# Two of the next four experts' activations placed between the value blocks of a dense expert stage

## The chip, the cores and the metric

The kernel runs on one core of one Trainium2 chip. The metric is device time in microseconds (us) of one execution. Before the change the median of three runs is 3982.32 us (3981.56 to 3986.05).

## The reference

One inference layer over nine blocks of 128 tokens (eight of a prompt, one of eight sampled sequences of 16 tokens): a mixer and then PEER, an expert layer of 16384 single-neuron experts. Only PEER's second half is touched by the change. For each token, 8 heads choose 16 experts each by product keys, and

```
u_sel = expert_u[e_idx]
act = gelu(einsum('thkd,td->thk', u_sel, xt))
out = einsum('thk,thkd->td', g * act, expert_v[e_idx])
```

with g the softmax of the 16 chosen scores. The mixer's recurrent half has a causal convolution and a scan, whose states of the sampled sequences come in as inputs (st_conv, st_lru) and go out updated (conv_s, lru_s).

## The kernel before, in words

The nine blocks are computed in three groups (mixer, scores, choice of experts), up to about 2010 us. Then PEER is done in two ways at once. Four blocks are *gathered*: for each of 128 choices, GpSimd issues an indirect transfer of one row of expert_u or expert_v per token (line 910), and VectorE reduces it (lines 937, 958). Five blocks are *dense*: all 16384 experts are computed for their 640 tokens, with a table G of weights that is zero where an expert was not chosen. The 16384 experts are 128 rows of 128; in the code, and in what follows, such a row of 128 is "an expert e" of the dense stage, and four of them (ECH) are a chunk c; there are 32 chunks.

The dense stage (function dense) has two pieces per chunk.

- u_phase(e, gt) is one activation. It loads expert_u's weights into raw, splits them into a high and a low half (hi on ScalarE, lo on VectorE: fp32 products are made of three matmuls), makes 2 x 24 matmuls into two PSUM tiles pp, applies gelu into wf (ScalarE, line 1043), multiplies by the weights in gt (VectorE, line 1045), and splits the result into wh (ScalarE) and wl (VectorE). wf has one buffer, wh and wl have five each (ECH + 1), gt has one buffer: the gt of a chunk can be loaded only when the fourth activation of the chunk before has been multiplied.
- v_phase(c, ws, vs) is the value product of a chunk, for the five token blocks in the order 2, 0, 3, 1, 4: 24 matmuls each (four experts, three products, two halves of 512 columns). Blocks 0 and 1 keep their sums in PSUM over the whole stage. Blocks 2, 3 and 4 share the one PSUM tile that is left, and after each of them VectorE adds the tile to acc (line 1077), which frees it. load_v(e) loads and splits an expert's values into vh and vl (four buffers each), which are free again when the last block of a chunk has read them.

Before the change the program's order per chunk is: activations 2 to 4 of the chunk, each followed by load_v; load_g of the next chunk; the first activation of the next chunk; v_phase; load_v for that first one.

The program's order is not the order on the engines. The Tile framework plans it beforehand (line 1280): on each engine, what comes first in the program has priority, and where that is not ready by the planner's reckoning, later work is put in. On the chip each engine then goes strictly by this plan. The gathers come last in the program, so their vector operations stand where VectorE had a gap in the plan.

The two lines that decide the order between the chunks' pieces:

```
nxt = [u_phase((c + 1) * ECH, gt)]
v_phase(c, ws, vs, nf)
```

Of the kernel before, what the change touches and what calls it, by code (L numbers as in the profile page):

```python
# [10 lines left out]
F32 = mybir.dt.float32  # L11
# [47 lines left out]
ECH = 4  # L59
AT_ONCE = (0, 5)  # L60
LAG = 3
FLOW = ((0,) * 5, (0.2, 0.26, 0.26, 0.26, 0.26), (0.13, 0.26, 0.3, 0.26, 0.26))


# [5 lines left out]
def kernel(ctx, tc, a):  # L70
    nc = tc.nc
    V, S, P, T = nc.vector, nc.scalar, nc.gpsimd, nc.tensor

    const = ctx.enter_context(tc.tile_pool(name="const", bufs=1))
# [27 lines left out]
    h_last = const.tile([128, 8], F32, name="h_last")  # L102
    V.memset(xr_last, 0.0)
    V.memset(h_last, 0.0)
    st_conv = const.tile([128, 8, 8, 3], F32, name="st_conv")
    nc.scalar.dma_start(st_conv, a["st_conv"])
    st_lru = const.tile([128, 8, 8], F32, name="st_lru")
    nc.scalar.dma_start(st_lru, a["st_lru"])
    conv_s = const.tile([128, 8, 8, 3], F32, name="conv_s")
    rms = const.tile([128, NB], F32, name="rms")  # L110
    lru_s = const.tile([128, 8, 8], F32, name="lru_s")

    xt_d = {b: dr_p.tile([128, D], F32, name=f"xt_d{b}") for b in range(NB)}
    s_d = [dr_p.tile([8, 128, len(g), 2, 128], F32, name=f"s_d{n}") for n, g in enumerate(GROUPS)]
# [133 lines left out]
    def mixer(mp, gi, t0, xn):  # L248
# [5 lines left out]
        samp = SB in blocks  # L254
# [6 lines left out]
        left = [sum(p * w for p, w in zip(parts, PACE[gi]))]  # L261
# [4 lines left out]
        def pair(name):  # L266
            return mp["big"].tile([128, 2, KT, Tn], F32, name=name, tag="big")
# [21 lines left out]


        ol = pair("ol")

        def lru_in(c):
            ps = pj(("w_in", CX + c), xn)
# [56 lines left out]
        def lru_scan(c, gb, xc, tr, h, av):  # L351
            V.scalar_tensor_tensor(xc, xc, 0.5, tr, op0=ALU.mult, op1=ALU.mult)
            V.tensor_tensor_scan(h[:, 0:Tp], av[:, 0:Tp], xc[:, 0:Tp], h_last[:, c:c + 1],
                                 op0=ALU.mult, op1=ALU.add)
            V.tensor_copy(h_last[:, c:c + 1], h[:, Tp - 1:Tp])
            if samp:
                bs = xc[:, Tp:Tn].rearrange("p (s t) -> p s t", s=8)[:, :, 0:1]
                as_ = av[:, Tp:Tn].rearrange("p (s t) -> p s t", s=8)[:, :, 0:1]
                ah = sm_p.tile([128, 8, 1], F32, name="ah")
                V.tensor_tensor(ah, as_, st_lru[:, c].unsqueeze(2), op=ALU.mult)  # L360
                V.tensor_tensor(bs, bs, ah, op=ALU.add)
                V.memset(as_, 0.0)
                V.tensor_tensor_scan(h[:, Tp:Tn], av[:, Tp:Tn], xc[:, Tp:Tn], 0.0,
                                     op0=ALU.mult, op1=ALU.add)
                V.tensor_copy(lru_s[:, c].unsqueeze(2),
                              h[:, Tp:Tn].rearrange("p (s t) -> p s t", s=8)[:, :, 15:16])
            V.scalar_tensor_tensor(h, h, 0.5, gb, op0=ALU.mult, op1=ALU.mult)
            split(ol[:, 0, c, :], ol[:, 1, c, :], h)

        ahead = deque([lru_in(0), lru_in(1)])  # L370
        for c in range(0, KT, 2):
            sts = []
            for e in range(2):
                if c + e + 2 < KT:
                    ahead.append(lru_in(c + e + 2))
                gb = lru_gelu(c + e)
                sts.append((gb, *lru_gates(c + e, *ahead.popleft())))
            for st in sts:
                S.activation(st[2], st[2], ACTF.Sqrt)
            for e in range(2):  # L380
                lru_scan(c + e, *sts[e])

        stage[0] = phase[1] = 1

# [633 lines left out]
    def dense(dp):  # L1018
        nd = len(DENSE)
        Td = nd * 128  # L1020
        xt2 = dp["x"].tile([128, 2, KT, Td], F32, name="xd")
        accs = [None, None]
        for i, b in enumerate(DENSE):
            x = (w_p.tile([128, D], F32, name="xt", tag="raw", bufs=RAW_BUFS) if i < RAW_BUFS else
                 w_p.tile([128, D], F32, name="xt", tag="lo"))
            nc.sync.dma_start(x, xt_d[b])
            transpose_in(x, xt2, i * 128, dp["ps"])

        ps_p = dp["pp"]
        ps_s = dp["ps"]  # L1030

        def u_phase(e, gt):
            tick(2)
            hi, lo = load_split(a["peer_ut"][e], raw=u0 if e == 0 else None)
            wh = dp["w"].tile([128, Td], F32, name="wh")
            wl = dp["w"].tile([128, Td], F32, name="wl")
            w = dp["w"].tile([128, Td], F32, name="wf", bufs=1)
            for m in range(0, Td, Td // 2):
                c1 = slice(m, m + Td // 2)
                ps = ps_p.tile([128, Td // 2], F32, name="pp", tag="pp")  # L1040
                for k in range(KT):
                    mm3(ps, (hi[:, k, :], lo[:, k, :]), (xt2[:, 0, k, c1], xt2[:, 1, k, c1]), k == 0, k == KT - 1)
                S.activation(w[:, c1], ps, ACTF.Gelu_apprx_tanh)  # L1043
            w3 = w.rearrange("p (c t) -> p c t", t=32)
            V.tensor_tensor(w3, w3, gt[:, :, e % ECH, :], op=ALU.mult)  # L1045
            split(wh, wl, w)
            return wh, wl

        def load_v(e):
            vh = dp["v"].tile([128, D], F32, name="vh")  # L1050
            vl = dp["v"].tile([128, D], F32, name="vl")
            return load_split(a["peer_v"][e], vh, vl, (128, D))

        def load_g(c):
            gt = dp["g"].tile([128, NCH, ECH, 32], F32, name="gt")
            nc.sync.dma_start(gt, G_d[:, :, c * ECH:(c + 1) * ECH, :].rearrange("n p i t -> p n i t"))
            return gt

        kept = [ps_s.tile([128, 2, 512], F32, name="S", tag="S") for _ in range(2)]

        def v_phase(c, ws, vs, nf=None):
            for i in (2, 0, 3, 1, 4):
                held = i < len(kept)
                po = kept[i] if held else ps_s.tile([128, 2, 512], F32, name="S", tag="S")
                c1 = slice(i * 128, i * 128 + 128)
                for n, ((wh, wl), (vh, vl)) in enumerate(zip(ws, vs)):
                    for q, (l, r) in enumerate(((wh, vh), (wh, vl), (wl, vh))):
                        for m in range(2):
                            T.matmul(po[:, m, :], r32(l[:, c1]), r32(r[:, m * 512:m * 512 + 512]),  # L1069
                                     start=(n == 0 and q == 0 and (c == 0 or not held)),  # L1070
                                     stop=(n == ECH - 1 and q == 2 and (c == nch - 1 or not held)))
                if held and c == nch - 1:
                    acc = w_p.tile([128, D], F32, name="acc", tag="lo")
                    nc.sync.dma_start(acc, x2_d[DENSE[i]])
                    accs[i] = acc
                if not held or c == nch - 1:
                    V.tensor_tensor(accs[i], accs[i], po.rearrange("p m c -> p (m c)"), op=ALU.add)  # L1077
                if c == nch - 1:
                    finish(DENSE[i], accs[i], w_p.tile([128, D], F32, name="yo", tag="hi"), nf)

        nch = 128 // ECH
        gt = load_g(0)
        ws, vs = [u_phase(0, gt)], [load_v(0)]
        for i in range(2, nd):
            acc = dp["x"].tile([128, D], F32, name=f"acc{i}")
            nc.sync.dma_start(acc, x2_d[DENSE[i]])
            accs.append(acc)
        for c in range(nch):
            for e in range(c * ECH + 1, (c + 1) * ECH):
                ws.append(u_phase(e, gt))  # L1090
                vs.append(load_v(e))
            nxt = []
            if c + 1 < nch:
                gt = load_g(c + 1)
                nxt = [u_phase((c + 1) * ECH, gt)]
            nf = None
            if not nxt:
                nf = w_p.tile([128, D], F32, name="nf", tag="raw", bufs=RAW_BUFS)
                nc.sync.dma_start(nf, a["norm_final"].to_broadcast([128, D]))
            v_phase(c, ws, vs, nf)  # L1100
            ws = nxt
            vs = [load_v((c + 1) * ECH)] if nxt else []

    mp = {nm: es_m.enter_context(tc.tile_pool(name=nm, bufs=bufs, reuse_waits="tile"))
          for nm, bufs in (("big", 2), ("s", S_BUFS), ("kv", 2), ("b", 2), ("c", 4))}
# [67 lines left out]
    es_m.close()  # L1173
    with ExitStack() as es:
        dp = {nm: es.enter_context(tc.tile_pool(name=f"d{nm}", bufs=bufs, reuse_waits="tile"))
              for nm, bufs in (("x", 1), ("w", ECH + 1), ("v", ECH), ("g", 1))}
        for nm, bufs in (("pp", 2), ("ps", 3)):
            dp[nm] = es.enter_context(tc.tile_pool(name=f"d{nm}", bufs=bufs, space=bass.MemoryType.PSUM))
        phase[0] = 3
        dense(dp)  # L1180
# [2 lines left out]
            pass  # L1183
    nc.sync.dma_start(a["conv_p"], xr_last)
    nc.sync.dma_start(a["lru_p"], h_last)
    nc.sync.dma_start(a["conv_s"], conv_s)
    nc.sync.dma_start(a["lru_s"], lru_s)


def layout(inp):  # L1190
# [109 lines left out]
```

## Time and profile before

| | before |
|---|---|
| median of three runs | 3982.32 us |
| profiled execution | 3979.21 us, span 3977.3 us |
| TensorE (PE) busy | 3647.0 us, 92% |
| VectorE (DVE) busy | 3042.7 us, 77% |
| ScalarE (ACT) busy | 1618.2 us, 41% |
| GpSimd (POOL) busy | 1405.4 us, 35% |
| moved by DMA | 1208.05 MB, mean 304 GB/s |

Times in a profile are microseconds from the first instruction. L1077 is line 1077 of the kernel. A matmul's busy time overlaps the next one's, so rates of TensorE are read from starts. "idle before <- X" names what ended the idle time: the work or transfer X that the engine waited for. PEclk is the mean clock granted to TensorE as a share of full speed.

### The profile page before, as it was taken

How to read it: one execution, taken by the hardware profiler on the slowest of the kernel's cores; microseconds unless marked ns; L12 is line 12 of the kernel's file. 1: busy time of each engine (PE TensorE's matmuls, PEld its weight loads, DVE VectorE, ACT ScalarE, POOL GpSimd, SP SyncE). 2: the span in 40 equal slices, each digit the busy share in tenths (PEclk: the TensorE clock that was granted, in tenths of full speed). 3: DMA queues.
4: the chain of work that ended last, by engine and by line, in shares of the span. 5: the costliest groups of instructions: out<-in, count | busy, mean ns of one | idle time of the engine just before them, and what ended most of it. 6: DMA issues, size and time to landing. Idle time of an engine off the chain costs nothing. (4 is left out here: it accounts for less than half of the span.)

```text
span 3977.3 us, 59539 instructions
## 1 busy us (share of the span) xinstructions
PE 3647.0 (92%) x21775; PEld 3264.7 (82%) x21775; DVE 3042.7 (77%) x6332; ACT 1618.2 (41%) x2699; POOL 1405.4 (35%) x1094
## 2 busy tenths in 40 slices
PE   8998899898998999888888889999999899999998
PEld 7877799876887987778888778888888888888887
DVE  8433357868675879987778888888877887877887
ACT  7554346556644845665532122222222222222222
POOL 0000000122221023222106555655664655655653
PEclk9999999999998999999999999999999999999999
DMA  7778887888899898879968888989888889888986
GB/s 260 253 243 317 296 283 271 327 308 269 316 385 331 294 346 292 292 281 360 379 203 308 306 287 296 320 314 343 311 305 293 322 313 332 311 304 305 331 311 233
DMA packets 470358, 1208.05 MB, mean 304 GB/s; under 512 B 41008, under 2 KB 199088, under 8 KB 467504
## 3 DMA queue, kind: packets, MB, share of 16 engines
q1 hardware_dynamic: 292496, 638.23, 45.2%
q0 software_dynamic: 147456, 536.94, 37.8%
q10 hardware_dynamic: 30112, 29.09, 2.1%
q8 instruction: 170, 2.79, 0.3%
q14 instruction: 124, 1.02, 0.1%
HBM read 1066.15 MB, written 137.94 MB: 303 GB/s over the span
## 5 line engine op out<-in xcount | busy, mean ns | idle before, releaser
L910 POOL DMA_INDIRECT row<-peer_u,ei x512 | 698.0, 1363 | 1260.5 <-DVE row L937 631.3
L910 POOL DMA_INDIRECT row<-peer_v,ei x512 | 683.3, 1334 | 828.7 <-DVE x L958 525.4
L958 DVE SCALAR_TENSOR_TENSOR x<-row,q,x 128x1024 f32<-128x1024 f32 x512 | 655.3, 1280 | 27.2 <-DMA row<-peer_v,ei 20.8
L175 PE MATMUL pp<-xd,hi 128*128 128x320 f32 x2048 | 639.8, 312 | 31.9 <-ACT wf L1043 26.9
L937 DVE SCALAR_TENSOR_TENSOR row<-row,xt 128x1024 f32<-128x1024 f32 x512 | 613.6, 1217 | 66.1 <-DMA row<-peer_u,ei 64.4
L176 PE MATMUL pp<-xd,hi 128*128 128x320 f32 x2048 | 637.5, 311 | 0.3 <-DVE xd L142 0.3
L177 PE MATMUL pp<-xd,lo 128*128 128x320 f32 x2048 | 636.8, 311 | 0.0
L175 PE MATMUL pp<-xn,hi 128*128 128x384 f32 x1344 | 477.4, 356 | 19.1 <-ACT st L1011 7.8
L1069 PE MATMUL S<-vh,wh 128*128 128x512 f32 x1280 | 410.0, 402 | 62.2 <-DVE acc L1077 54.0
L177 PE MATMUL pp<-xn,lo 128*128 128x384 f32 x1344 | 459.4, 343 | 2.1 <-DMA lo<-lo_w_in 2.1
L176 PE MATMUL pp<-xn,hi 128*128 128x384 f32 x1344 | 460.6, 343 | 0.1
L1069 PE MATMUL S<-vh,wl 128*128 128x512 f32 x1280 | 401.1, 402 | 27.6 <-DVE wl L142 27.6
L175 PEld LDWEIGHTS pp<-xd,hi 128*128 128x128 f32 x2048 | 389.9, 190 | 42.6 <-ACT wf L1043 30.7
L141 ACT CAST hi<-raw 128x1024 fp32r<-128x1024 f32 x223 | 233.8, 1049 | 429.0 <-PE pp L176 307.2
L1069 PE MATMUL S<-vl,wh 128*128 128x512 f32 x1280 | 404.0, 397 | 0.0
L176 PEld LDWEIGHTS pp<-xd,hi 128*128 128x128 f32 x2048 | 389.8, 190 | 7.2 <-DVE xd L142 0.6
L177 PEld LDWEIGHTS pp<-xd,lo 128*128 128x128 f32 x2048 | 389.2, 190 | 1.6
L142 DVE TENSOR_TENSOR lo<-raw,hi 128x1024 fp32r<-128x1024 f32 x223 | 271.9, 1220 | 150.1 <-ACT hi L141 134.8
L141 ACT CAST wh<-wf 128x640 fp32r<-128x640 f32 x128 | 93.3, 729 | 616.8 <-DVE wf L1045 583.6
L1069 PEld LDWEIGHTS S<-vh,wh 128*128 128x128 f32 x1280 | 239.3, 193 | 112.3 <-DVE acc L1077 60.9
L163 ACT CAST hi<-raw 128x1024 fp32r<-128x1024 f32 x192 | 200.4, 1047 | 296.5 <-PE pp L176 204.3
L1069 PEld LDWEIGHTS S<-vh,wl 128*128 128x128 f32 x1280 | 246.7, 194 | 84.6 <-DVE wl L142 32.7
(296 smaller groups left out, 6821.7 us busy)
## 6 DMA issues: line engine op xcount, KB each, us to landing
raw<-w_in SPq DMA_DIRECT2D x168, 512.0 KB
raw<-peer_v SPq DMA_DIRECT2D x128, 512.0 KB
raw<-peer_ut SPq DMA_DIRECT2D x127, 512.0 KB
lo<-lo_w_in SPq DMA_DIRECT2D x112, 512.0 KB
G_d<-st SPq DMA_DIRECT2D x20, 2048.0 KB
gt<-G_d SPq DMA_DIRECT2D x32, 1280.0 KB
lo_w_in<-lo SPq DMA_DIRECT2D x56, 512.0 KB
raw<-wq SPq DMA_DIRECT2D x48, 512.0 KB
```

What stands on the lines that cost most here:

```text
L141: S.copy(r32(hi), src)
L142: ins = V.tensor_tensor(r32(lo), src, hi, op=ALU.subtract)
L163: S.copy(r32(hi), raw)
L175: T.matmul(out, r32(lh), r32(rh), start=first, stop=False)
L176: T.matmul(out, r32(lh), r32(rl), start=False, stop=False)
L177: T.matmul(out, r32(ll), r32(rh), start=False, stop=last)
L910: P.indirect_dma_start(out=t, out_offset=None, in_=table, in_offset=bass.IndirectOffsetOnAxis(ap=ei[:, j:j + 1], axis=0))
L937: V.scalar_tensor_tensor(u, u, 1.0, xt, op0=ALU.mult, op1=ALU.mult, accum_out=hh[:, j:j + 1])
L958: V.scalar_tensor_tensor(x2, v, q[:, j:j + 1], x2, op0=ALU.mult, op1=ALU.add)
L1069: T.matmul(po[:, m, :], r32(l[:, c1]), r32(r[:, m * 512:m * 512 + 512]), start=(n == 0 and q == 0 and (c == 0 or not held)), stop=(n == EC ...
```

## The change

The activations of the next chunk are spread. v_phase becomes a generator that yields after each token block. After its second block (MIDST's key 1) and after its fourth (key 3) one activation of the next chunk is written; the two others follow the fifth block, mixed with the loads of the four value pairs: load, load, activation, load, load, activation. load_g of the next chunk stands ahead of the blocks. The buffers of wh and wl go from five to six. To make room, the states of the convolution and the scan (st_conv, st_lru, conv_s, lru_s) leave the pool of constants for a pool that lives only during the first group's mixer; they are loaded there, and stored right after its scan instead of at the program's end.

```
+MIDST = {1: 1, 3: 1}
...
-    st_conv = const.tile([128, 8, 8, 3], F32, name="st_conv")
-    nc.scalar.dma_start(st_conv, a["st_conv"])
...
+        if samp:
+            st_conv = mp["q"].tile([128, 8, 8, 3], F32, name="st_conv", bufs=1)
+            nc.scalar.dma_start(st_conv, a["st_conv"])
...
+        if samp:
+            nc.sync.dma_start(a["conv_s"], conv_s)
+            nc.sync.dma_start(a["lru_s"], lru_s)
...
+        for e in range(1, ECH):
+            ws.append(u_phase(e, gt))
+            vs.append(load_v(e))
         for c in range(nch):
-            for e in range(c * ECH + 1, (c + 1) * ECH):
-                ws.append(u_phase(e, gt))
-                vs.append(load_v(e))
-            nxt = []
-            if c + 1 < nch:
+            more = c + 1 < nch
+            nf = None
+            if more:
                 gt = load_g(c + 1)
-                nxt = [u_phase((c + 1) * ECH, gt)]
...
-            v_phase(c, ws, vs, nf)
-            ws = nxt
-            vs = [load_v((c + 1) * ECH)] if nxt else []
+            nxt = []
+            for k, _ in enumerate(v_phase(c, ws, vs, nf)):
+                for _ in range(MIDST.get(k, 0) if more else 0):
+                    nxt.append(u_phase((c + 1) * ECH + len(nxt), gt))
+            ws, vs = nxt, []
+            if more:
+                left = ECH - len(ws)
+                for k in range(ECH):
+                    vs.append(load_v((c + 1) * ECH + k))
+                    while ECH - len(ws) > left - (left * (k + 1)) // ECH:
+                        ws.append(u_phase((c + 1) * ECH + len(ws), gt))
...
-              for nm, bufs in (("x", 1), ("w", ECH + 1), ("v", ECH), ("g", 1))}
+              for nm, bufs in (("x", 1), ("w", ECH + 2), ("v", ECH), ("g", 1))}
```

## Rows read from the trace of the kernel before

**Rows 1.** Busy time by stretch: engines, granted clock, DMA share, GB/s.
```profile
500.00:1000.00 500.00, 464.40 (x2698) 412.63 (x2697) 376.53 (x1278) 286.28 (x510) 73.50 (x70) 0.97 0.83 290
2100.00:2400.00 300.00, 251.65 (x1326) 224.71 (x1325) 266.38 (x632) 60.93 (x87) 172.43 (x124) 0.95 0.86 302
2400.00:3900.00 1500.00, 1438.79 (x7889) 1300.92 (x7888) 1240.62 (x1429) 373.50 (x525) 897.50 (x624) 0.98 0.88 314
```
**Rows 2.** Timeline of SyncE's queue: start, us, instruction; issues of gt.
```profile
2273.60 0.38 SPq L1056 DMA_DIRECT2D gt<-G_d  x1
...
3830.70 0.38 SPq L1056 DMA_DIRECT2D gt<-G_d  x1
...
3892.39 0.38 SPq L1056 DMA_DIRECT2D gt<-G_d  x1
```
**Rows 3.** Timeline of TensorE, 2960 to 2991 us.
```profile
2960.74 0.63 PE L1069 MATMUL S<-vh,wh 128*128 128x512 f32 x2
...
2966.22 0.31 PE L177 MATMUL pp<-xd,lo 128*128 128x320 f32 x1
...
2977.48 0.31 PE L175 MATMUL pp<-xd,hi 128*128 128x320 f32 x1
...
2990.54 0.31 PE L177 MATMUL pp<-xd,lo 128*128 128x320 f32 x1
2990.68 0.63 PE L1069 MATMUL S<-vh,wh 128*128 128x512 f32 x2
```
**Rows 4.** Waits of TensorE, 2010 us to the end: us, times, longest.
```profile
PE S L1069 <- DVE acc L1077: 54.0, 24, 6.7
PE S L1069 <- DVE wl L142: 27.6, 12, 4.2
PE pp L175 <- ACT wf L1043: 26.9, 9, 7.7
PE S L1069 <- ACT wh L141: 7.5, 5, 3.6
PE pp L175 <- ACT hi L141: 3.9, 1, 3.9
```
**Rows 5.** Waits of VectorE, 2010 us to the end.
```profile
DVE wf L1045 <- DMA gt<-G_d: 195.6, 28, 9.2
DVE row L937 <- DMA row<-peer_u,ei: 46.2, 44, 4.3
```
**Rows 6.** Timeline of TensorE in one chunk, 3826 to 3859 us.
```profile
3827.42 0.31 PE L177 MATMUL pp<-xd,lo 128*128 128x320 f32 x1
...
3835.63 0.31 PE L177 MATMUL pp<-xd,lo 128*128 128x320 f32 x1
...
3858.32 1.22 PE L1069 MATMUL S<-vh,wh 128*128 128x512 f32 x2 [4.08 <-DVE acc L1077]
```
**Rows 7.** Timeline of VectorE: an earlier chunk's end, then the same chunk.
```profile
3001.79 0.82 DVE L142 TENSOR_TENSOR wl<-wf,wh 128x640 fp32r<-128x640 f32 x1
...
3829.85 0.82 DVE L1045 TENSOR_TENSOR wf<-wf,gt 128x640 f32<-128x640 f32 x1
...
3831.78 0.81 DVE L142 TENSOR_TENSOR wl<-wf,wh 128x640 fp32r<-128x640 f32 x1
...
3850.53 0.83 DVE L1045 TENSOR_TENSOR wf<-wf,gt 128x640 f32<-128x640 f32 x1 [8.75 <-DMA gt<-G_d]
...
3857.05 1.22 DVE L1077 TENSOR_TENSOR acc<-acc,S 128x1024 f32<-128x1024 f32 x1
```
**Rows 8.** Groups of instructions by line, 2100 to 3900 us: busy us, mean ns.
```profile
L142 DVE TENSOR_TENSOR lo<-raw,hi 128x1024 fp32r<-128x1024 f32 x120 | 146.2, 1219 | 33.5 <-ACT hi L141 33.2
L142 DVE TENSOR_TENSOR vl<-raw,vh 128x1024 fp32r<-128x1024 f32 x117 | 141.1, 1217 | 2.4 <-ACT vh L141 2.3
```
**Rows 9.** Waits of ScalarE, 2010 us to the end.
```profile
ACT vh L141 <- DMA raw<-peer_v: 81.1, 26, 5.7
```
**Rows 10.** Timeline of ScalarE's queue, the first us.
```profile
4.44 0.33 ACTq L106 DMA_DIRECT2D st_conv<-st_conv  x1
6.78 0.33 ACTq L108 DMA_DIRECT2D st_lru<-st_lru  x1
```
**Rows 11.** Timeline of VectorE: the last gathered block's norm.
```profile
3948.04 1.28 DVE L905 SCALAR_TENSOR_TENSOR x<-x,rs_rg,yf 128x1024 f32<-128x1024 f32 x1 [0.72 <-DMA yf<-norm_final]
```

More of the change, by code (lines that the diff above doesn't have):

```diff
@@ L104 @@
     V.memset(h_last, 0.0)
-    st_conv = const.tile([128, 8, 8, 3], F32, name="st_conv")
-    nc.scalar.dma_start(st_conv, a["st_conv"])
-    st_lru = const.tile([128, 8, 8], F32, name="st_lru")
-    nc.scalar.dma_start(st_lru, a["st_lru"])
-    conv_s = const.tile([128, 8, 8, 3], F32, name="conv_s")
     rms = const.tile([128, NB], F32, name="rms")
-    lru_s = const.tile([128, 8, 8], F32, name="lru_s")
     xt_d = {b: dr_p.tile([128, D], F32, name=f"xt_d{b}") for b in range(NB)}
@@ L291, in mixer @@
         ol = pair("ol")
+        if samp:
+            st_conv = mp["q"].tile([128, 8, 8, 3], F32, name="st_conv", bufs=1)
+            nc.scalar.dma_start(st_conv, a["st_conv"])
+            st_lru = mp["q"].tile([128, 8, 8], F32, name="st_lru", bufs=1)
+            nc.scalar.dma_start(st_lru, a["st_lru"])
+            conv_s = mp["q"].tile([128, 8, 8, 3], F32, name="conv_s", bufs=1)
+            lru_s = mp["q"].tile([128, 8, 8], F32, name="lru_s", bufs=1)
         def lru_in(c):
@@ L1079, in v_phase @@
                     finish(DENSE[i], accs[i], w_p.tile([128, D], F32, name="yo", tag="hi"), nf)
+                yield
         nch = 128 // ECH
@@ L1087, in dense @@
             accs.append(acc)
+        for e in range(1, ECH):
+            ws.append(u_phase(e, gt))
+            vs.append(load_v(e))
         for c in range(nch):
-            for e in range(c * ECH + 1, (c + 1) * ECH):
-                ws.append(u_phase(e, gt))
-                vs.append(load_v(e))
-            nxt = []
-            if c + 1 < nch:
+            more = c + 1 < nch
+            nf = None
+            if more:
                 gt = load_g(c + 1)
-                nxt = [u_phase((c + 1) * ECH, gt)]
-            nf = None
-            if not nxt:
+            else:
                 nf = w_p.tile([128, D], F32, name="nf", tag="raw", bufs=RAW_BUFS)
                 nc.sync.dma_start(nf, a["norm_final"].to_broadcast([128, D]))
-            v_phase(c, ws, vs, nf)
-            ws = nxt
-            vs = [load_v((c + 1) * ECH)] if nxt else []
+            nxt = []
[9 more added lines that the diff above has]
+                        ws.append(u_phase((c + 1) * ECH + len(ws), gt))
     mp = {nm: es_m.enter_context(tc.tile_pool(name=nm, bufs=bufs, reuse_waits="tile"))
@@ L1185 @@
     nc.sync.dma_start(a["lru_p"], h_last)
-    nc.sync.dma_start(a["conv_s"], conv_s)
-    nc.sync.dma_start(a["lru_s"], lru_s)
 def layout(inp):
```

## The prediction

> **What bounds the kernel now.** I read the stretches first, then the waits of the two busiest engines over the dense stage, then one chunk instruction by instruction.
>
> The stretches [rows 1] show that the change lies in the second half. From 2010 us to the end only the dense stage and the row gathers run. Between 2400 and 3900 us TensorE is busy 1438.79 of 1500 us, VectorE 1240.62 (83%), the DMA engines 0.88. No engine is full, so I look at what stops TensorE. A period of a chunk (four experts) comes from the issues of the tile gt: 27 of them from 2273.60 to 3892.39 us, 59.96 us each [rows 2]. Against it stands TensorE's own work. An activation of one expert is 48 matmuls; 90 of them start in the 13.20 us from 2977.48 to 2990.68, 146.7 ns apart, so one u_phase is 7.04 us. A block of the value product is 24 matmuls, 2960.74 to 2966.22, so 5.48 us [rows 3]. Four u_phases and five blocks are 28.2 + 27.4 = 55.6 us. So each chunk loses about 4.4 us.
>
> TensorE's waits over the dense stage [rows 4] name VectorE each time: 54.0 us until an add into acc has freed the PSUM buffer of a block, 27.6 us for wl, 26.9 us for gelus, which themselves wait for the one buffer wf. VectorE's own waits [rows 5] say why it is late: 195.6 us, in 28 chunks of 32, it stands at the multiply by gt, and everything queued behind stands with it.
>
> One chunk shows the chain. The last activation's matmuls end at 3827.73 [rows 6]. Its multiply at 3829.85 frees gt [rows 7], SyncE issues the next gt at 3830.70 [rows 2]. The first activation of the next chunk ends on TensorE at 3835.94 [rows 6], but its multiply starts at 3850.53, after 8.75 us of an idle VectorE [rows 7]: gt takes 19.8 us. Behind it in the same queue is the add of block 2, at 3857.05, and TensorE, having run out of other work, stands 4.08 us until 3858.32 [rows 6]. A short stall is followed by a second loss, the clock: granted 0.95 in the first 300 us and 0.98 after [rows 1], so 0.05 x 300 + 0.02 x 1500 = 45 us of full-speed time went at its lower level (1.2 instead of 2.4 GHz).
>
> **The change part by part.** No matmul, vector instruction or dense transfer is added or removed; they are moved.
>
> *Activations between the blocks.* The first two activations of the next chunk now stand behind blocks 0 and 1. Blocks 2, 3 and 4 share one PSUM buffer, so between the reader of one and the writer of the next stand a block and an activation, 5.48 + 7.04 = 12.5 us, where one block, 5.48 us, stood. The shown lateness of the add, 8.75 us of stall and a few operations, fits into this. I take the whole 54.0 us as gone (bounds 0 and 54.0).
>
> *gt.* It is still issued 3.0 us behind the end of the last activation and lands 19.8 us later, at 22.8 us. Its first user now comes behind two blocks and its own matmuls, 5.48 + 5.48 + 7.04 = 18.0 us, plus the 2.1 us from matmul to multiply (3827.73 to 3829.85): 20.1 us. The stall falls from 8.75 to about 2.7 us, over 31 chunks from 195.6 to 84 us. VectorE per chunk: 49.6 us of work (1240.62 x 59.96 / 1500), 2.7 for gt, 1.5 for rows not landed (46.2 / 31 [rows 5]), 53.8 us in all, below TensorE's 55.6. So TensorE is late next. The 26.9 us behind wf lie in the chunks before 2400 us, where the selection of the gathered blocks fills VectorE to 266.38 of 300 us; with the gt stall out and that work still there I take half, 13 us (bounds 0 and 26.9).
>
> *Clock.* 67 of the 124 us of TensorE waits go; I let the 45 us shrink less than in proportion, by 20 us (bounds 0 and 45).
>
> *The end of a chunk loses its cover.* Until now the first activation of the next chunk, 7.04 us, stood between the last activation and the value blocks. Now block 2 follows at once. Its first three experts, 18 matmuls, and four matmuls with wh cover 22 x 0.228 = 5.0 us before wl is needed. The chain from the last matmul to the end of wl took 2990.85 to 3002.61, 11.8 us [rows 3, 7], in the first of 15 successive chunk ends and 3827.73 to 3832.59, 4.9 us [rows 6, 7], in the last; ten of them take 4.8 to 4.9, five 7.4 to 11.8, mean 6.5. Queued behind a waiting matmul is all of block 2, and nothing waits for VectorE meanwhile. The mean exceeds the cover by 1.5 us, 46 us in 31 chunk ends; half of that I put down to today's 27.6 us for wl and 7.5 for wh [rows 4], so I take 23 us more. Bounds: 35 us less, if today's waits go too, and 6.8 x 31 = 211 us more, if every end is as the worst.
>
> *Values loaded behind the last block.* All four pairs are freed by block 4, as before, but now 14.1 us of activations follow it, not 28.2. In that time VectorE has four vl and two lo at 1.22, three multiplies and splits at 0.82 + 0.82, one add at 1.21: 13.4 us [rows 7, 8]. ScalarE waits at most 5.7 us for a landed value [rows 9]. The four raw buffers hold the first values early; the last activation's weights are asked for only when a value has left its buffer. I take 0.3 us per chunk, 10 us (bounds 0, since no large wait of TensorE names a value or a weight today [rows 4], and 5.7 x 31 = 177 us).
>
> *Six buffers, and the small states.* The sixth pair lets both activations be written while four are read; without it the second would wait for block 4 and the order above could not hold. The states of the convolution and the scan move from the constants into the mixer: two loads of 0.33 us each on ScalarE's queue, the first at 4.44 us [rows 10], and two stores on SyncE's queue that now stand behind the mixer's scan. Their cover is the wait for the first x; without it they cost their issue, under 2 us. I take nothing.
>
> Sum: -54 - 13 - 20 + 23 + 10 = -54 us. The profiled execution took 3979.21 us (span 3977.3), the median of the runs is 3982.32; I take the same off both: 3928 us.
>
> **Rivals.**
> *The cover is what mattered (slower).* wf is one buffer, so the last activation's gelu waits for the split of the one before, and both now stand right behind the loads of four values, on a VectorE that has 13.4 of 14.1 us taken. If gathered rows get between, more ends look like the late one. It cancels the gain when the mean chain passes 5.0 + 77 / 31 = 7.5 us. With 60% late ends it is 9.0 us: 4.0 x 31 = 124 us against 77, so 3982 + 47 = 4029. For it: 5 of 15 ends are late today. Against it: ten are not, with gathered rows all around them.
>
> *The order stays what it was.* The program's order is only a wish; the planner fills waits on TensorE with what is ready, and activations already run among the blocks today (2966.22 begins inside one [rows 3]). Then gt stalls as before: 3975 to 3990.
>
> *The bunched weights.* If the last activation's weights come 2 to 2.5 us late each chunk, 62 to 77 us go again: about 3985.
>
> *The gathers end last.* The last gathered block's norm ends at 3949.3 [rows 11], 28 us ahead of the end of the span. If the gathers keep their pace while the dense stage gets shorter, they end the kernel: at most 28 us are gained, and with the store behind the norm about 22: 3960. For it: a row's issue on GpSimd took 73.50 / 70 = 1.05 us where VectorE was busy 75%, and 897.50 / 624 = 1.44 us at 83% [rows 1]. Against it: GpSimd has 40% idle, and the rows stand in VectorE's queue between the dense work, so they are drawn along.
> The Trainium skill ("SBUF — State Buffer", section "SBUF: two separate sides") has a rule behind that row: a vector operation that holds the port pair shared with GpSimd shuts GpSimd out, and transfers issued from there starve for descriptors. By that rule a denser VectorE (86% where 83% was) would add, on the line through the two stretches, about 0.15 us to each of the 624 issues, an estimate of 90 us within 600 us of idle GpSimd: it does not bind, but it speaks for this rival.
>
> *All of it goes.* 54.0 + 26.9 + 45, and nothing new at the chunk ends: 126 us less, 3856.
>
> **How the numbers follow.** Forecast 45%, lost cover 22%, unchanged order 10%, gathers last 9%, all gone 8%, bunched weights 6%. No change means within 0.2%, 8 us, which is about what a measurement of this kernel can tell. Faster are the forecast, the gathers and the full gain, 62%, and a little of the bunched weights: 0.63; the same are the unchanged order and part of the weights: 0.13; slower 0.24. The range takes in the larger part of the full gain and the milder half of the lost cover: 3868 to 3998. The forecast's own range is 3890 to 3958.
>
> **What would show it.** Right: VectorE's wait for gt near 85 us, TensorE's wait for acc under 10 us, period of gt issues near 57.5 us, clock at 0.98 to 0.99. TensorE's wait for wl and wh would be near 58 us; above 110 us the slower rival holds. Waits of TensorE for hi, vh or vl above 40 us would be the bunched weights. If the order on TensorE still has acc waits of 50 us, the planner undid the change. A last row behind the last block of values would be the gathers.

## The result, and the profile after

The changed kernel takes 4015.16 us (median of 5 runs, 4003.6 to 4020.75), the kernel before 3982.32 in the same comparison (5 runs, 3976.21 to 3986.31). The ratio is 1.0075 [1.0052, 1.0098]: 33 us more, where 54 less were forecast. The profiled execution took 4020.75 us with a span of 4019.0, 41.7 longer than before's 3977.3.

First the two dense stretches of the changed kernel (columns as in [rows 1]), then the fifth issue of gt and the last, which answer to [rows 2].
```profile
2100.00:2400.00 300.00, 241.34 (x1240) 212.24 (x1239) 260.19 (x605) 57.45 (x81) 179.74 (x130) 0.92 0.86 303
2400.00:3900.00 1500.00, 1424.49 (x7791) 1283.55 (x7790) 1217.38 (x1414) 366.29 (x517) 857.44 (x609) 0.98 0.87 308
```
```profile
2289.78 0.38 SPq L1061 DMA_DIRECT2D gt<-G_d  x1
...
3931.15 0.38 SPq L1061 DMA_DIRECT2D gt<-G_d  x1
```
Count the matmuls: from 2400 to 3900 us 7791 were done where before did 7889, and from 2100 to 2400 us 1240 against 1326. In the long stretch TensorE's granted clock is the same (0.98 in both), so there it stands idle more; in the short one the clock is lower too, 0.92 where it was 0.95. The time sits in four places. The dense stage starts 7 us later; its first four periods take 9 us more; from the fifth to the last issue a period is (3931.15 - 2289.78) / 27 = 60.79 us where it was 59.96, 23 us in all; the tail takes 3 more. The 7 us are no effect that I could show: the first issue of gt came at 2007.38 us in before and at 2014.47 after, and in the experiments below at 2008 to 2017 where the small states lie as before, at 2008 to 2025 where they were moved.

The waits from 2010 us to the end: TensorE's (against [rows 4]), VectorE's ([rows 5]), ScalarE's ([rows 9]), and two of ScalarE's before.
```profile
PE S L1075 <- DVE acc L1083: 61.5, 31, 5.6
PE pp L170 <- ACT wf L1048: 23.1, 8, 6.8
PE pp L170 <- ACT hi L136: 21.8, 8, 5.7
PE S L1075 <- ACT wh L136: 18.6, 9, 3.4
PE S L1075 <- DVE wl L137: 14.9, 4, 5.9
PE S L1075 <- DVE vl L137: 4.2, 4, 3.0
```
```profile
DVE wf L1050 <- DMA gt<-G_d: 214.4, 27, 9.4
DVE row L942 <- DMA row<-peer_u,ei: 40.9, 34, 6.1
```
```profile
ACT hi L136 <- DMA raw<-peer_ut: 147.7, 54, 7.5
ACT vh L136 <- PE S L1075: 73.1, 43, 7.0
ACT vh L136 <- DMA raw<-peer_v: 5.6, 1, 5.6
```
```profile
ACT vh L141 <- PE S L1069: 138.3, 69, 10.1
ACT hi L141 <- DMA raw<-peer_ut: 48.7, 18, 8.9
```
Two things are to be seen. Both waits that the change should have removed are there, and longer: gt 214.4 us (195.6), acc 61.5 (54.0). And a third has tripled: ScalarE stands 147.7 us for activation weights that have not landed, where it stood 48.7 us before, and TensorE 21.8 us for hi (3.9). Values hardly ever come late now (5.6 against 81.1): they wait ready in the raw buffers, and the weights come late instead.

One chunk shows that the order on TensorE is not the one that the program asks for. TensorE, then VectorE, from 3629 to 3660 us:
```profile
3629.45 1.09 PE L1075 MATMUL S<-vh,wl 128*128 128x512 f32 x4
3630.37 0.31 PE L170 MATMUL pp<-xd,hi 128*128 128x320 f32 x1
...
3636.24 0.31 PE L171 MATMUL pp<-xd,hi 128*128 128x320 f32 x1
3636.39 0.63 PE L1075 MATMUL S<-vh,wh 128*128 128x512 f32 x2
...
3657.51 1.22 PE L1075 MATMUL S<-vh,wh 128*128 128x512 f32 x2 [2.87 <-DVE acc L1083]
```
```profile
3632.36 0.82 DVE L1050 TENSOR_TENSOR wf<-wf,gt 128x640 f32<-128x640 f32 x1
...
3639.55 1.22 DVE L1083 TENSOR_TENSOR acc<-acc,S 128x1024 f32<-128x1024 f32 x1
...
3652.48 0.82 DVE L1050 TENSOR_TENSOR wf<-wf,gt 128x640 f32<-128x640 f32 x1 [8.06 <-DMA gt<-G_d]
...
3656.24 1.22 DVE L1083 TENSOR_TENSOR acc<-acc,S 128x1024 f32<-128x1024 f32 x1
```
The multiply at 3632.36 frees gt and SyncE issues the next one at 3633.20. By the program two blocks, 48 matmuls, should stand between the chunk's last activation and the next chunk's first. Four stand there, those at 3629.45; the first activation is on TensorE from 3630.37. Its multiply waits 8.06 us for gt, the add into acc stands behind it, and TensorE waits 2.87 us. That is the picture of [rows 6, 7].

The other chunks are like it. Counted over the 31 chunk ends of the trace, 9 value matmuls stand there on average, where before had 15 (its median is 3, the changed kernel's 12). From the end of the last activation to the end of the next chunk's first it takes 11.4 us; before it took 11.5.

### The profile page after: what moved, and what is told of

Its sections match the earlier page's. It is cut to its first block, busy times and chain, and to the rows that moved or that the text cites. A ratio compares the mean times of both kernels' runs of the same rounds, so it can differ in the third digit from the quotient of the medians.

```text
span 4019.0 us, 59486 instructions
## 1 busy us (share of the span) xinstructions
PE 3671.2 (91%) x21775; PEld 3277.5 (82%) x21775; DVE 3045.8 (76%) x6332; ACT 1620.2 (40%) x2699; POOL 1399.6 (35%) x1094
## 5 line engine op out<-in xcount | busy, mean ns | idle before, releaser
L1075 PE MATMUL S<-vh,wh 128*128 128x512 f32 x1280 | 415.6, 407 | 80.3 <-DVE acc L1083 61.5
L1075 PE MATMUL S<-vh,wl 128*128 128x512 f32 x1280 | 399.2, 401 | 14.9 <-DVE wl L137 14.9
```

## The experiments

Two theories went in: the order is undone by the planner, which fills TensorE's waits with whatever is ready; and the loads bunched behind the last block ("the bunch") cost the time. Edits are against the changed kernel unless it says "before".

**Room alone.** Before with the changed kernel's buffers and its place for the small states, the dense order untouched:
```diff
-    st_conv = const.tile([128, 8, 8, 3], F32, name="st_conv")
...
+            st_conv = mp["q"].tile([128, 8, 8, 3], F32, name="st_conv", bufs=1)
...
-              for nm, bufs in (("x", 1), ("w", ECH + 1), ("v", ECH), ("g", 1))}
+              for nm, bufs in (("x", 1), ("w", ECH + 2), ("v", ECH), ("g", 1))}
```


> The old order of the dense stage, with the new six buffers of wh and wl and the states in the mixer's pool. Theory 1 (the loss lies in the new order: values and weights asked for in a bunch, the planner pulling the next activation forward as before): 3982 within 8 us, VectorE's wait for gt near 195 us, TensorE's wait for hi near 4 us. Rival (the sixth buffer or the moved states shift the plan by themselves): 3995 to 4015, with the dense stage starting some 7 us later.


3983.66 against 3979.63 us, ratio 1.0000 [0.998, 1.002]. Six buffers and the moved states cost nothing that can be seen.

**Five buffers with the new order.**
```diff
-              for nm, bufs in (("x", 1), ("w", ECH + 2), ("v", ECH), ("g", 1))}
+              for nm, bufs in (("x", 1), ("w", ECH + 1), ("v", ECH), ("g", 1))}
```


> The new order with five buffers of wh and wl. Theory 1: about the changed kernel, 4015 within 10 us, as only one activation is ever ahead in the plan. Rival (the sixth buffer carries the order, and without it the second activation stands behind the last block): 4030 or more, with TensorE's waits for wh and wl above 60 us.


4027.93 us, ratio 1.0118 [1.0089, 1.0147]; waits for gt 211.6, acc 69.2 us, ScalarE's for weights 157.2. That is 3 us above what I expected, and the rival's sign, wh and wl above 60 us, is not there (33.8). The loss is there without the sixth buffer too, and its interval overlaps that of the change: it lies in the new order of activations and loads.

**The order tied on TensorE.** Each activation between the blocks is held until the last matmul of the block ahead of it has been issued:
```diff
-                            T.matmul(po[:, m, :], r32(l[:, c1]), r32(r[:, m * 512:m * 512 + 512]),
+                            last_mm[0] = T.matmul(po[:, m, :], r32(l[:, c1]), r32(r[:, m * 512:m * 512 + 512]),
...
-                    nxt.append(u_phase((c + 1) * ECH + len(nxt), gt))
+                    with tc.issue_after(last_mm[0].ins):
+                        nxt.append(u_phase((c + 1) * ECH + len(nxt), gt))
```


> The changed kernel, but the matmuls of the two activations in the middle are tied behind the last matmul of the block that precedes them in the program, so the planner cannot pull them forward. Theory 1: VectorE's wait for gt falls from 214 to about 85 us, TensorE's wait for acc from 61 to under 15, and the time to 3930 to 3960. Rival (the chunk's end loses its cover): the first block of a chunk now waits on wh, wl and vl for over 110 us together, and the time is 4015 or more.


3999.97 us, ratio 1.0031 [1.0009, 1.0052]. The mechanism of the forecast appears in part (gt 119.1, wf 1.1 us), and so does its price, as TensorE's waits show:
```profile
PE S L1077 <- ACT wh L136: 60.3, 19, 6.6
PE S L1077 <- DVE acc L1085: 26.9, 15, 4.1
```
wl adds 19.5 us and hi stays at 15.0. Tying alone gives back some 15 us; the time is far from the 3930 to 3960 expected, and the kernel is still not faster than before.

**The loads spread.** Each value is loaded behind its own activation again; the order of the activations is the changed kernel's:
```diff
+                    nvs.append(load_v((c + 1) * ECH + len(nvs)))
+            ws, vs = nxt, nvs
+            while more and len(ws) < ECH:
+                ws.append(u_phase((c + 1) * ECH + len(ws), gt))
+                vs.append(load_v((c + 1) * ECH + len(vs)))
```


> The changed kernel, but each of the four value loads follows its own activation in the program instead of all standing behind the last block. Theory 1: TensorE's wait for hi falls from 22 to about 5 us and ScalarE's wait for landed weights from 148 to about 50, time 3990 to 4000. Rival (the loads' place is harmless): 4015 within 8 us and the same waits.


3967.54 us, ratio 0.9972 [0.9954, 0.999]. This one edit takes the ratio from 1.0075 to 0.9972, some 41 us of 3980 (48 between the two medians), more than I expected. Its waits, TensorE's and ScalarE's:
```profile
PE pp L170 <- ACT wf L1048: 53.7, 20, 9.8
PE S L1075 <- DVE acc L1083: 26.3, 16, 3.2
```
```profile
ACT hi L136 <- DMA raw<-peer_ut: 78.2, 32, 6.7
```
hi is at 4.0 us on TensorE, and the wait for weights is halved, while gt (175.6) is still late. So it was the place of the loads that turned a small gain into a loss. The edit changed the order on TensorE as well, though nothing is tied: 31 value matmuls now stand at a chunk's end where 9 stood.

**Both.** The two edits together:
```diff
+                    with tc.issue_after(last_mm[0].ins):
+                        nxt.append(u_phase((c + 1) * ECH + len(nxt), gt))
+                    nvs.append(load_v((c + 1) * ECH + len(nvs)))
```


> Both edits of the two last better runs: the middle activations tied behind their blocks, and each value load behind its own activation. Theory 1 (two separate faults: loads in a bunch, and the pulling forward): gt's wait near 120 us as when tied alone, TensorE's wait for hi near 4 us, acc under 27, time 3945 to 3960. Rival (the chunk's end without cover eats what tying gives): TensorE's waits for wh and wl stay at 60 us or more, time 3967 or above.


3963.36 against 3976.94 us, ratio 0.9959 [0.9944, 0.9974], not to be told from the spread loads alone. It lies just above the 3945 to 3960 expected. The program that my prediction described, with the loads behind the last block, is the tied one alone, at 3999.97. With the loads spread, what the forecast said of the order can be read without the bunch. Waits (TensorE's, then VectorE's) and stretches:
```profile
PE S L1077 <- ACT wh L136: 40.3, 15, 6.9
PE S L1077 <- DVE acc L1085: 27.8, 13, 5.0
PE S L1077 <- DVE wl L137: 17.9, 7, 4.1
PE pp L170 <- ACT hi L136: 4.0, 1, 4.0
```
```profile
DVE wf L1050 <- DMA gt<-G_d: 97.4, 20, 8.0
```
```profile
2100.00:2400.00 300.00, 248.78 (x1274) 216.75 (x1274) 288.86 (x683) 62.54 (x87) 195.41 (x141) 0.90 0.93 327
2400.00:3900.00 1500.00, 1464.00 (x8132) 1328.11 (x8131) 1264.12 (x1429) 386.29 (x542) 896.59 (x625) 0.99 0.89 319
```
Its period from the fifth to the last issue is (3860.13 - 2289.66) / 27 = 58.17 us, and the profiled span 3946.2, 31 less than before's (the medians differ by 14). After 2400 us it does 8132 matmuls where before did 7889: 243 more, at 5.26 per us 46 us gained. From 2100 to 2400 us it does 52 fewer, 12 us lost: there VectorE is busy 288.86 of 300 us, and of the 58.2 us for wh and wl 50.2 stand ahead of 2400 us. The lost cover is paid there, and hardly at all later.

**gt in two halves, on before.** Two tiles of half the table in the same memory, so that the first half can be refilled while the second is used:
```diff
-            gt = dp["g"].tile([128, NCH, ECH, 32], F32, name="gt")
-            nc.sync.dma_start(gt, G_d[:, :, c * ECH:(c + 1) * ECH, :].rearrange("n p i t -> p n i t"))
-            return gt
+            gts = []
+            for h in range(2):
+                gt = dp["g"].tile([128, NCH, 2, 32], F32, name="gt", bufs=2)
+                e0 = c * ECH + 2 * h
+                nc.sync.dma_start(gt, G_d[:, :, e0:e0 + 2, :].rearrange("n p i t -> p n i t"))
+                gts.append(gt)
+            return gts
```


> The kernel before, with gt as two tiles of two experts each (two buffers, the same memory): the first half is free two activations earlier, so it can land before it is needed. Packets are half as long. Theory 1 (the stall on gt is what makes VectorE late, and so the waits for acc and wf): VectorE's wait for gt under 50 us instead of 196, TensorE's waits for acc and wf together under 40 instead of 81, time 3900 to 3940. Rival (VectorE is full anyway, the stall is only where its idle time shows): the wait for gt goes but waits for rows take its place, time 3975 to 3990.


3933.47 us, ratio 0.9895 [0.9871, 0.9919]: better than both kernels, and the lowest median of the study. TensorE's waits from 2010 us on fall from 122.0 to 19.7 us, that for acc from 54.0 to 0.4. The last value matmul, then the gathered rows' last group of adds:
```profile
3818.49 0.61 PE L1073 MATMUL S<-vh,wl 128*128 128x512 f32 x2
```
```profile
3920.76 3.93 DVE L958 SCALAR_TENSOR_TENSOR x<-row,q,x 128x1024 f32<-128x1024 f32 x3 [0.82 <-DMA row<-peer_v,ei]
```
Groups of instructions from 3819 to 3926 us:
```profile
L958 DVE SCALAR_TENSOR_TENSOR x<-row,q,x 128x1024 f32<-128x1024 f32 x68 | 87.3, 1283 | 11.2 <-DMA row<-peer_v,ei 9.7
L910 POOL DMA_INDIRECT row<-peer_v,ei x64 | 78.3, 1224 | 24.3 <-issue 16.2 <-DVE x L958 3.0 <-DVE rs_m L122 1.5
```
The dense product ends 148 us earlier than before (3966.9 there) and the kernel only 43: the rows were left behind, 68 adds at 107 / 68 = 1.57 us each, with TensorE empty.

**Halves with spread loads.** The table's edit on the kernel with the loads spread.
```diff
-            V.tensor_tensor(w3, w3, gt[:, :, e % ECH, :], op=ALU.mult)
+            V.tensor_tensor(w3, w3, gt[e % ECH // 2][:, :, e % 2, :], op=ALU.mult)
```


> The new order with spread value loads, and gt in two halves. Theory 1: as for the kernel before, a gain of 40 to 80 us on the 3968 of the spread loads, so 3890 to 3930. Rival (VectorE full, or transfers at their limit with the shorter packets): 3960 or more.


3950.34 us, ratio 0.9927 [0.991, 0.9943]: short of what I expected. TensorE waits only 14.9 us, the last value matmul is at 3823.3, but 75 rows come behind it, the last at 3939.9.

**Bunching alone, on before.** From the second chunk on, all four values are loaded ahead of its last three activations:
```diff
+                if c:
+                    vs.append(load_v(e))
+            for e in range(c * ECH + 1, (c + 1) * ECH):
                 ws.append(u_phase(e, gt))
-                vs.append(load_v(e))
+                if c == 0:
+                    vs.append(load_v(e))
```


> The kernel before, with only the place of the value loads changed: from the second chunk on, all four of a chunk stand ahead of the three activations that follow the value blocks, not one behind each activation. Theory 1 (the bunched loads are the fault by themselves, since values that wait for the last block fill the four raw buffers): slower, 4000 to 4040, with ScalarE's wait for landed activation weights above 120 us instead of 49 and TensorE's wait for hi above 15 instead of 4. Rival (they only hurt together with activations in the middle): 3980 within 8 us.


4272.26 us, ratio 1.074 [1.0714, 1.0765]: 295 us, far more than expected. ScalarE's waits, then TensorE's:
```profile
ACT vh L141 <- PE S L1069: 391.4, 120, 15.6
ACT hi L141 <- DMA raw<-peer_ut: 151.2, 62, 8.7
```
```profile
PE S L1069 <- DVE acc L1077: 203.3, 49, 12.1
PE pp L177 <- DVE lo L142: 56.5, 23, 7.1
PE pp L175 <- ACT hi L141: 43.0, 24, 5.2
```
In ScalarE's plan the casts of four values stand first until the last block has freed the pairs, 391.4 us in all (138.3 before), and the cast of the next weight is behind them. On TensorE a chunk's second activation comes late: it starts after 136 value matmuls counted from the start of the chunk before it, that is behind all 120 of that chunk; before it started after 74.

**Tied, spread and halved.** All three edits; the tie again:
```diff
+                    with tc.issue_after(last_mm[0].ins):
+                        nxt.append(u_phase((c + 1) * ECH + len(nxt), gt))
```


> Three edits together: middle activations tied behind their blocks, value loads behind their own activations, gt in two halves. In the tied order the last gathered row was used 60 us ahead of the last block, so the gathers have room to end last later. Theory (the dense stage and the gathers now each set the end, whichever is later): dense stage ending near 3840, gathers near 3870, time 3880 to 3920, below all others. Rival (the gathers' vector operations take the same clock time whatever the dense stage does): 3935 to 3955, as in the other two kernels with halves.


3954.76 us, ratio 0.9933 [0.9913, 0.9954], far from the 3880 to 3920 of the theory and inside the rival's 3935 to 3955. The reason is that of the two halved kernels above: the last value matmul at 3853.1, 58 rows behind it, the last at 3943.5.

**Halves on the changed kernel.** Only the table is split:
```diff
-            return gt
+            return gts
```


> The changed kernel with gt in two halves and nothing else. Theory (two separate faults, the stall on gt and the bunched value loads): VectorE's wait for gt goes, TensorE's waits for acc and wf nearly too, but its waits for hi, lo and wh stay at 30 to 50 us; the last block ends 20 us or more later than the 3823 of the spread loads with halves. Rival (the bunched loads only hurt through the stall on gt): the last block ends at 3825 within 8 us.


3939.79 us, ratio 0.991 [0.9887, 0.9933], not to be told from the halves on before. I expected more harm from the bunch. TensorE's longest waits are now
```profile
PE S L1079 <- ACT wh L136: 8.7, 2, 8.4
PE pp L172 <- DVE lo L137: 8.3, 2, 4.7
```
and the last value matmul, at 3829.4, is 6 us behind that with the loads spread. So the rival held: in this order the bunch hurts only together with the stall on gt. The two are not separate faults. Only 3 value matmuls stand at a chunk's end here, and that does no harm once gt is there in time.

**Raw buffers of their own for the values**, with five pairs and the new order (second experiment), so that a waiting value holds no buffer that a weight needs. One of the two is taken from the gathered rows, which keep five of six:
```diff
-ROW_BUFS = (3, 6)
+ROW_BUFS = (3, 5)
...
-            return load_split(a["peer_v"][e], vh, vl, (128, D))
+            if e % 2:
+                raw = g_p.tile([128, D], F32, name="rg", tag="g5")
+            else:
+                raw = dp["v"].tile([128, D], F32, name="rv", bufs=1)
+            nc.sync.dma_start(raw, a["peer_v"][e])
+            return load_split(None, vh, vl, (128, D), raw=raw)
```


> The new order with five buffers of wh and wl (4028 us), but the raw values have two buffers of their own (one of them from the gathered rows, which keep five of six), so activation weights alone use the four raw buffers. Theory (values that wait for the last block hold the raw buffers, and the activations' weights are asked for too late): ScalarE's wait for landed activation weights falls from 157 to under 60, TensorE's wait for hi from 14 to about 4, time 3975 to 4000. Rival (it is the place of the value splits in the queues of ScalarE and VectorE, not the buffers): 4020 or more.


3996.22 us, ratio 1.0056 [1.003, 1.0083], where the same order without it was at 1.0118. ScalarE's wait for weights, 157.2 us there, is gone; hi on TensorE falls from 14.3 to 2.7 us, acc from 69.2 to 12.8, VectorE's wait for gt from 211.6 to 100.5. The value matmuls at a chunk's end go from 9 to 34. What remains is wf on TensorE:
```profile
PE pp L170 <- ACT wf L1048: 89.5, 36, 6.9
```
The edit has prices of its own: ScalarE waits 132.9 us for landed values (5.5), and VectorE 184.7 us for rows (68.4).

**The same buffers on the bunched before.**
```diff
+            if e % 2:
+                raw = g_p.tile([128, D], F32, name="rg", tag="g5")
+            else:
+                raw = dp["v"].tile([128, D], F32, name="rv", bufs=1)
```


> The kernel before with all four value loads bunched (4272 us), but raw values in two buffers of their own as in the run beside it. Theory (buffers): most of the 295 us goes, 4000 to 4080, TensorE's waits for hi and lo fall from 100 to under 25. Rival (queues): 4200 or more, and TensorE's wait for acc stays near 200.


4013.25 us, ratio 1.0088 [1.0068, 1.0109], from 1.074: 259 of the 295 us were in the raw buffers, and the second activation is back among the blocks (after 77 value matmuls). Both runs give separate buffers and more of them, six in place of four; six shared ones were not tried. ScalarE's wait, then TensorE's two:
```profile
ACT vh L141 <- PE S L1074: 187.9, 55, 10.1
```
```profile
PE S L1074 <- DVE acc L1082: 94.1, 26, 6.6
PE pp L175 <- ACT hi L141: 2.7, 1, 2.7
```

## Why the prediction was wrong

Two steps failed. Forecast and result lie 87 us apart, 54 less and 33 more.

**The first: "Values loaded behind the last block".** I priced it at 10 us, from the waits that TensorE had before. But before had no bunch, so its rows could not show one. In the runs the place of the loads is worth some 41 us: 31 of the 87, and more than the whole loss. The mechanism is the one I named (values hold the raw buffers, weights are asked for late), and the two runs with buffers of their own bear it out: with ScalarE's wait for weights gone, 32 us come back on the new order and 259 on the old one. A second side I left out: a value's cast that stands first in ScalarE's plan holds up what is behind it. It shows where the bunch was put on before (391.4 us of waits for blocks); in the changed kernel it does not (73.1 us, 138.3 before). Nor is the 41 us a price of the bunch by itself, since with gt in halves 6 us of it are left. My upper bound, 177 us, did cover 41; choosing 10 was the error.

**The second: "Activations between the blocks" and "gt".** Both worked out times along the program's order: the next chunk's first activation behind two blocks, done 18.0 us after the last one. In the changed kernel it is done 11.4 us after it. So acc took 61.5 us where I had put nothing, gt 214.4 where I had put 84, and the 54, 13 and 20 us for acc, wf and clock were not had. The rival "the order stays what it was" described the trace. Means over the 31 chunk ends of each trace:

| kernel | value matmuls between a chunk's last activation and the next one | us from the end of the one to the end of the other | VectorE's wait for gt, us |
|---|---|---|---|
| forecast | 48 | 18.0 | 84 |
| before | 15 | 11.5 | 195.6 |
| changed | 9 | 11.4 | 214.4 |
| new order, five pairs | 9 | 11.6 | 211.6 |
| the same, raw buffers of their own | 34 | 17.4 | 100.5 |
| loads spread | 31 | 17.1 | 175.6 |
| tied | 38 | 18.8 | 119.1 |
| tied and spread | 51 | 20.9 | 97.4 |

The two steps hang together. With the loads spread, or with raw buffers of their own for the values, the order comes much nearer to the program's, though nothing is tied. The place of a chunk's fourth activation moves with it: in the changed kernel it starts when 21 value matmuls of its own chunk have started (before: 24), with the loads spread 9, with the buffers 2 (20 without them). What TensorE does ahead of the late activation is then missing behind it.

Tied and spread, the kernel does much of what these steps say: gt 97.4 us for 84, wf 0.8 for the half of 26.9. But the acc wait was over-credited: 26.2 of 54.0 went, not all, and with the loads spread and nothing tied it is as low (26.3), so that this part is not shown to come from the order.

**"The end of a chunk loses its cover".** Right in kind where the order holds: wh and wl 58.2 us with the loads spread, as forecast, and 79.8 tied alone. It did not grow into the slower rival, which needed more than 110. That the size met 58 is in part luck. I had spread it over all chunk ends, from 15 that begin at 2990 us; most of it falls before 2400 us. There before's own trace had longer chains: its first six ends, up to 2400 us, take 8.7 to 28.0 us from the last matmul to the end of wl.

**Clock.** In the tied and spread kernel it rose from 0.98 to 0.99 after 2400 us and fell from 0.95 to 0.90 before, 15 us each way by the forecast's own rule (0.01 x 1500, 0.05 x 300): the 20 us credited came to nothing. With the 27.8 us of acc waits that makes 48 us of credit that was not there to be had, against 13 more than forecast at wf. Without the bunch's 10 us the forecast is 64; 29 of it remain. The profiled span of this kernel is 31 us shorter than before's, its median 14.

**The rivals.** Unchanged order and bunched weights came together; I had given 16% to the two, as separate cases that end near no change. The slower rival was overpriced: 9.0 us takes every late end as the worst, 11.8; with the mean of the five late ends, 9.8, it is 7.8 us, and the time 3992 instead of 4029. That 4015 lies near 4029 says nothing for it: in the changed kernel TensorE waits 33.5 us for wh and wl, no more than before (35.1). Gathers that end last did decide, but only once the table was split: 148 us less of dense stage bought 43.

**Other readings.** The rows of TensorE's waits do not all name VectorE: wf, wh and hi, 38.3 us of 122.0, are ScalarE's. And 45 us is the full-speed time that the clock cost; at half speed that is 90 us spent at the lower level.

Left open: why the changed kernel's stall for gt is slightly longer than before's; what the remaining 33 us of the bunch with its own buffers are (the casts' place in ScalarE's plan fits 187.9 us of waits, but no run moved them alone); why gt still waits 175.6 us with the loads spread, though the next activation comes later; and where the last rows would have to be issued for the dense gain to be kept.

## What to carry to other kernels

Where a planner may reorder an engine, a new program order is a hypothesis: read the engine's timeline before pricing it. Before loads are moved together, ask which buffer a loaded tile holds while it waits for its target, and who else draws from that set: a late load also changes what the planner puts in its place. A wait on one buffer that is refilled whole can be cheaper to remove by splitting the buffer than by moving work around it; then look for what ends last.

## What the runs showed of the hardware

Splitting gt halves the contiguous pieces that the transfer reads, from 512 to 256 bytes. The shorter pieces cost engine time. The queue that carries gt, before and split on before (packets, MB, share of the 16 DMA engines' span):
```profile
q1 hardware_dynamic: 292496, 638.23, 45.2%
q1 hardware_dynamic: 374928, 638.23, 47.2%
```
Of spans of 3977.3 and 3934.7 us these shares are 1798 and 1857 us for the same bytes; the ten kernels with whole tables lie between 1795 and 1809, the four with halves between 1847 and 1857. From 2100 to 3950 us a packet of 256 bytes took 20.4 ns on average, one of 512 bytes 28.9. From 2400 to 3900 us the engines were busy 0.91 where they were 0.88, at 315 GB/s instead of 314. The Trainium skill ("DMA: Bandwidth & Descriptors", section "Specifications") asks for 512 bytes for the full rate; this trace agrees in that two short packets take 40.8 ns where one long one takes 28.9. No delay of it shows: a half landed 9.6 us after its issue (median), and no wait of VectorE for gt was left.

At the end of that kernel, with TensorE done, gathered rows still came no faster than one in 1.57 us, while VectorE's add takes 1.283 us and an issue on GpSimd 1.224.

In the prediction I drew a line through two stretches, by which GpSimd's issues grow with VectorE's share. It does not hold: at the end of the split kernel, from 3819 to 3926 us, VectorE was busy 94.57 / 107 = 88% and an issue took 1.224 us, where the line gives 1.7; in the tied and spread kernel from 2100 to 2400 us VectorE was busy 96% and an issue took 195.41 / 141 = 1.39 us, where it gives 2.1. [rows 1] had the answer: from 2100 to 2400 us 172.43 / 124 = 1.39 us at 89%. The rule that I put beside it (the Trainium skill, "SBUF — State Buffer", section "SBUF: two separate sides") speaks of which instructions hold the shared port, not of a share of busy time; no run here took the instructions apart.
